# Two-layer hybrid decoder trunk on one core: the SBUF buffers get new start addresses

## The chip, the cores and the metric

The kernel runs on one core of a Trainium2 chip. The metric is the device time of one execution in microseconds (us). Two runs of the kernel before took 2884.22 and 2880.01 us, median 2882.11 us. A further, profiled execution took 2881.91 us, and its trace covers a span of 2880.1 us from the first to the last instruction.

## The reference

Two layers, sequence 256, model width 2048, everything in float32. Cut to what is computed:

```python
for l in range(2):
    u = rms_norm(x, g_mix[l])
    cq, ckv, xb, yb, gate_a, gate_r = split_columns(u @ w_in[l])   # 512, 576, 4 x 2048 columns
    attn = mla_branch(cq, ckv, ...)        # 16 heads, low-rank q and kv, rotary part, causal
    rec = rglru_branch(xb, yb, ...)        # conv4, 16 block-diagonal gates, linear scan, gelu
    x = x + (sigmoid(gate_a) * attn + sigmoid(gate_r) * rec) @ w_out[l]
    x = x + square(relu(rms_norm(x, g_mlp[l]) @ w_up[l])) @ w_down[l]      # 2048 -> 8192 -> 2048
    x = x + sigmoid(rms_norm(x, g_ple[l]) @ w_ple_gate[l]) * (p[l] @ w_ple_proj[l])
return rms_norm(x, g_final)
```

## The kernel before, in words

**Layout.** Activations stay in SBUF transposed: feature on the partition, the 256 positions along the free axis. `x` is `[128, 16, 256]` float32, 16 KiB a partition. `bufA` and `bufB` are `[128, 16, 2, 256]`, 32 KiB a partition each; index 2 chooses the high or the low part of an activation that was split in two (`hi` is the value rounded to the fp32r type, `lo` the remainder). They change roles from stage to stage: one holds the normalised input of a projection, the other the mixer's merged result or the MLP's hidden values.

**Weights.** The host lays all weights out as 1,004 "halves" of `[128, 1024]` float32. SyncE loads them in order into `raw` (6 buffers, lines 137 to 143). `split_half` (line 155) then makes two SBUF tiles of each: ScalarE copies `raw` into `hi` (line 160), VectorE computes `lo = raw - hi` (line 164). `hi` and `lo` have three buffers each, in the pool `wsp`. A half thus costs one ScalarE and one VectorE instruction, and feeds 24 matmuls.

**Products.** Each product of a weight block (the stationary operand, 128 columns, 512 bytes a partition) and an activation tile (the moving operand, 256 columns, 1,024 bytes a partition) is made as three fp32r matmuls: hi x hi, hi x lo, lo x hi. Two routines issue nearly all of them: `mm_both` (line 284 is its matmul; two output tiles at a time) and `mm3` (lines 259 to 261). Every matmul has a weight load of its own in front of it. Line 872 to 874 (the value projection `v`) is the one place where the roles are turned round: there the weights are the moving operand and the normalised latent `c1hi`/`c1lo` is the stationary one.

**Stages of a layer**, by the names that the trace shows as outputs: `c` and `kr` (the compressed q, kv and rope key), then eight head groups of `xb`, `yb`, `gr`, `k`, `v`, `q`, `qr`, `lru`, `ga` with the small attention matmuls `s` (scores), `pt` (transposes) and `o` (values) in between; `out`; four times `up` (16 tiles) and `down`; and `pg`/`pp`, the gated embedding. Between stages a norm issues a few matmuls of one column (`ms_...`, line 555) and one of 256 columns (`rb_...`, line 604).

**Order.** The program is emitted under a manual schedule: the order on each engine is fixed when the program is built, by a planner that carries costs of every step (`work`, `later`, `need`). Those costs do not depend on addresses.

**Where buffers lie.** Tile pools are placed one behind the other in the order in which they are opened, and the tiles of a pool in the order of their first allocation. Pool `const` comes first; its first tile starts at byte 16,512 of the partition, behind a reserved region and four small constants. So `x` starts at 16,512, and everything that follows takes its address from the sizes before it. All steps that the matmuls take from there (a tile of an activation 1,024 or 2,048 bytes, a block of a weight 512 bytes, a buffer 4,096 bytes) are multiples of 512 bytes, so an operand's address modulo 512 is that of its buffer.

Of the kernel before, what the change touches and what calls it, by code (L numbers as in the profile page):

```python
# [11 lines left out]
F32 = mybir.dt.float32  # L12
# [6 lines left out]
P = 128  # L19
S = 256  # L20
D = 2048
KT = D // P
DEPTH = 2
# [21 lines left out]
NPC = _c  # L45
# [8 lines left out]
def _parts(x, bits, n):  # L54

    out = []
    x = Fraction(x)
    for i in range(n):
        if x == 0:
            out.append(0.0)  # L60
            continue
        b = bits if i < n - 1 else 24
        m, e = math.frexp(float(x))
        q = Fraction(2) ** (e - b)
        v = Fraction(round(x / q)) * q
        out.append(float(v))
        x -= v
    return out


def _centered(x):
    x = x - math.floor(x)
    return x - 1 if x > Fraction(1, 2) else x
# [3 lines left out]
def trunk_kernel(ctx: ExitStack, tc: tile.TileContext, xT, pT, pos, par, gfin, invf, wu, out):  # L77
    nc = tc.nc

    const = ctx.enter_context(tc.tile_pool(name="const", bufs=1))  # L80
    wraw = ctx.enter_context(tc.tile_pool(name="wraw", bufs=6))
    wsp = ctx.enter_context(tc.tile_pool(name="wsp", bufs=3))
    tmp = ctx.enter_context(tc.tile_pool(name="tmp", bufs=6))
    att = ctx.enter_context(tc.tile_pool(name="att", bufs=1))
    tiny = ctx.enter_context(tc.tile_pool(name="tiny", bufs=4))
    banks = {
        t: (ctx.enter_context(tc.tile_pool(name=f"ps_{t}", bufs=n, space=PSUM)), n)
        for t, n in (("mm", 3), ("s", 2), ("t", 1), ("o", 1), ("r", 1))
# [120 lines left out]
    def later(key, *steps, deps=(), rank=1, also=()):  # L209

        job = Job((key, *also), rank, deps, steps)
        at = len(jobs)
        while at and jobs[at - 1].rank > rank:
            at -= 1
        jobs.insert(at, job)
# [126 lines left out]
        return tmp.tile([P, S], F32, tag="h", bufs=3, name=name)  # L342


    x = const.tile([P, KT, S], F32, name="x")

    bufA, bufB = (const.tile([P, KT, 2, S], F32R, name=n) for n in ("bufA", "bufB"))
    parT = const.tile([P, DEPTH * NPC], F32, name="parT")
    gf = const.tile([P, KT], F32, name="gf")
    nc.sync.dma_start(out=parT, in_=par)  # L350
    nc.sync.dma_start(out=x[:, 0:2, :], in_=xT[:, 0:2, :])
    load_to(0)
# [12 lines left out]
    make_identity(nc, ident)  # L365
    ones = const.tile([P, P], F32, name="ones")
    V.memset(ones, 1.0)
    power = const.tile([P, 4], F32, name="power")
    A.activation(power, ones[:, 0:4], AF.Copy, scale=-0.5)
    mask = const.tile([P, S], F32, name="mask")  # L370
    V.memset(mask[:, 0:P], 0.0)
# [2 lines left out]
    ropeS = const.tile([P, S], F32, name="ropeS")  # L374

    def rope_tables():
        fr = const.tile([P, 1], F32, name="invf")
        nc.sync.dma_start(out=fr, in_=invf)
        slots = []
        for n, tag in enumerate(("xch", "xcl", "vh", "vl")):  # L380
            w = att.tile([P, 512], F32, tag=tag, name=f"rope_w{n}")
            slots += [w[:, 0:S], w[:, S:512]]
        posi, ang, p2, p1, rem, turn, k, k2 = slots
        nc.sync.dma_start(out=posi.bitcast(I32), in_=pos.partition_broadcast(P))
        ops = []

        def ts(*a, **kw):
            ops.append(("V", 0.21, lambda: V.tensor_scalar(*a, **kw)))

        def tt(*a, **kw):  # L390
            ops.append(("V", 0.35, lambda: V.tensor_tensor(*a, **kw)))

        def rounded(o, src, by):
            ts(out=o, in0=src, scalar1=by, scalar2=ROUND, op0=ALU.mult, op1=ALU.add)
            ts(out=o, in0=o, scalar1=ROUND, scalar2=None, op0=ALU.subtract)

        def less(o, src, kk, c):
            ops.append(("V", 0.35, lambda: V.scalar_tensor_tensor(out=o, in0=kk, scalar=-c, in1=src, op0=ALU.mult, op1=ALU.add)))

        ops.append(("V", 0.21, lambda: V.tensor_copy(ang, posi.bitcast(I32))))  # L400
        ts(out=ang, in0=ang, scalar1=fr, scalar2=None, op0=ALU.mult)

        rounded(p2, ang, 2.0 ** -20)
        less(rem, ang, p2, 2.0 ** 20)
        rounded(p1, rem, 2.0 ** -10)
        less(rem, rem, p1, 2.0 ** 10)
        for n, (p, e) in enumerate(((p2, 20), (p1, 10))):
            c = _parts(_centered(Fraction(2) ** e / (2 * _PI)), 12, 3)
            if n == 0:
                ts(out=turn, in0=p, scalar1=c[0], scalar2=None, op0=ALU.mult)  # L410
            else:
                less(turn, turn, p, -c[0])
            rounded(k, turn, 1.0)
            less(turn, turn, k, 1.0)
            less(turn, turn, p, -c[1])
            less(turn, turn, p, -c[2])
        rounded(k, turn, 1.0)
        less(turn, turn, k, 1.0)
        c = _parts(2 * _PI, 12, 3)
        rounded(k2, rem, float(1 / (2 * _PI)))  # L420
        for v in c:
            less(rem, rem, k2, v)
        less(rem, rem, turn, -float(2 * _PI))
        rounded(k, rem, float(1 / (2 * _PI)))
        for v in c:
            less(rem, rem, k, v)
        ts(out=k, in0=rem, scalar1=3.1415925, scalar2=-3.1415925, op0=ALU.min, op1=ALU.max)

        ts(out=k2, in0=k, scalar1=-1.0, scalar2=None, op0=ALU.mult)
        tt(out=k2, in0=k, in1=k2, op=ALU.max)  # L430
        ts(out=k2, in0=k2, scalar1=-1.0, scalar2=math.pi / 2, op0=ALU.mult, op1=ALU.add)
        ops.append(("A", 1.0, lambda: A.activation(ropeS, k, AF.Sin)))
        ops.append(("A", 1.0, lambda: A.activation(ropeC, k2, AF.Sin)))

        for b in (0, 64):
            ts(out=ropeS[b:b + 32, :], in0=ropeS[b:b + 32, :], scalar1=-1.0, scalar2=None, op0=ALU.mult)
        later("rope", *ops, rank=1)


    cl = const.tile([P, DEPTH, 16], F32, name="cl")  # L440
    cl2 = const.tile([P, DEPTH, 16], F32, name="cl2")
    hba = const.tile([P, DEPTH, 16], F32, name="hba")
    hbx = const.tile([P, DEPTH, 16], F32, name="hbx")

    def lru_constants():
        work_ = t512("lru_c")
# [196 lines left out]

    PT = tuple(att.tile([P, 512], F32R, name=f"pt_{w}") for w in ("hi", "lo"))

    xbuf = att.tile([P, 2, 260], F32, name="xbuf")
    V.memset(xbuf[:, :, 0:4], 0.0)

    def split_steps(d, name, src, tag, cols=512):
# [35 lines left out]
    def mixer(l, u, mg, norm):  # L685
# [9 lines left out]
        for n in range(4):  # L695
            i, pr = divmod(n, 2)
            key = ("c", i, pr, l)
            ps = mm_pair(f"c{i}{pr}_{l}", key, u, hooks.get(n, ()))
            later(key, ("A", 0.6, lambda i=i, pr=pr, ps=ps: A.activation(dest(i, pr), ps, AF.Copy)), rank=-1)
            if l == n == 0:  # L700
                rope_tables()
                lru_constants()
            nl.squares((nl.name, "sq", n), lambda i=i, pr=pr: raw[i, pr], i, deps=(key,), last=pr == 1)
# [729 lines left out]
```

## Time and profile before

| | |
|---|---|
| median of 2 runs | 2882.11 us (2880.01 to 2884.22) |
| profiled execution | 2881.91 us, span 2880.1 us, mean granted TensorE clock 0.998 |
| TensorE matmul busy | 2853.1 us (99%), 24,800 matmuls |
| weight load busy | 2846.8 us (99%), 24,800 loads |
| VectorE busy | 1861.3 us (65%), 2,420 instructions |
| ScalarE busy | 1538.4 us (53%), 2,050 instructions |
| chain that ended last | 98% TensorE, 1% ScalarE |
| DMA | 535.43 MB, 186 GB/s, the weights' queue 55.6% of 16 engines' span |

How to read it: matmuls are pipelined and their ends are modelled, so that one is shown as 276 ns long while the next begins 113 ns after it. What a matmul costs the kernel is therefore the distance from its start to the next start, which this document calls the **step**. A window's count of matmuls gives it: a window of W us shows (W + 0.28) / step of them, since one that began up to 0.28 us before the window still reaches into it. The granted clock is a share of 2.4 GHz.

### The profile page before, as it was taken

Reading aid. Unit: us, or ns where it says so; the run is one execution under the profiler, and the core shown is the slowest. Engines: PE = TensorE matmul, PEld = TensorE weight load, DVE = VectorE, ACT = ScalarE, POOL = GpSimd, SP = SyncE. Lnnn points to the kernel's source line nnn. Section 1 sums busy time; section 2 is a strip of 40 time slices with the busy share of each in tenths; the row PEclk is TensorE's granted clock in tenths of the full one; section 3 lists DMA queues with packets and bytes.
Section 4 is the critical chain, followed back from the end, with each engine's and each line's share of the span. In section 5 each row is a group of like instructions: output and inputs, shape, how many; then the busy total and the mean of one; then the engine's idle time right before and its main releaser. Section 6 shows DMA issues by size and latency. Waiting matters only on the chain.

```text
span 2880.1 us, 60564 instructions
## 1 busy us (share of the span) xinstructions
PE 2853.1 (99%) x24800; PEld 2846.8 (99%) x24800; DVE 1861.3 (65%) x2420; ACT 1538.4 (53%) x2050; POOL 10.1 (0%) x17
## 2 busy tenths in 40 slices
PE   8999999999999999999999999999999999999998
PEld 8999999999999999999999999999999999999998
DVE  7877777765555555556758777777555555555665
ACT  5666666644444443444546666666453444434555
POOL 0000000000000000000000000000000000000000
PEclk9999999999999999999999999999999999999999
DMA  6555555555555555655555555555555555555553
GB/s 232 169 176 179 172 171 178 178 184 190 197 193 194 195 193 195 198 195 191 190 188 172 176 169 176 176 178 179 186 191 195 194 196 193 194 194 197 196 187 129
DMA packets 272583, 535.43 MB, mean 186 GB/s; under 512 B 30512, under 2 KB 30768, under 8 KB 272304
## 3 DMA queue, kind: packets, MB, share of 16 engines
q1 hardware_dynamic: 272304, 531.55, 55.6%
q8 instruction: 194, 3.18, 0.4%
q14 instruction: 85, 0.70, 0.1%
HBM read 529.33 MB, written 2.10 MB: 185 GB/s over the span
## 4 chain that ended last, share of the span: by engine, by line
PE 98%; ACT 1%; DVE 0%; DMA 0%; issue 0%; SPq 0%; ACTq 0%; POOLq 0%
PE up L284 24%; PE down L284 21%; PE yb L284 6%; PE gr L284 6%; PE xb L284 6%; PE out L284 5%; PE pg L284 5%; PE ga L284 5%; PE c L284 3%; PE down L259 1%; PE down L260 1%; PE down L261 1%; PE o L1040 1%; PE s L984 1%; PE v L872 1%; PE v L873 1%
## 5 line engine op out<-in xcount | busy, mean ns | idle before, releaser
L160 ACT ACTIVATE hi<-raw 128x1024 fp32r<-128x1024 f32 x1004 | 1065.7, 1061 | 1311.6 <-DMA raw<-wu 467.4
L164 DVE TENSOR_TENSOR lo<-raw,hi 128x1024 fp32r<-128x1024 f32 x1004 | 1229.5, 1225 | 808.1 <-ACT hi L160 786.0
L284 PE MATMUL up<-bufA,hi 128*128 128x256 f32 x2048 | 316.2, 276 | 0.0
L284 PE MATMUL up<-bufB,hi 128*128 128x256 f32 x2048 | 316.2, 276 | 0.0
L284 PE MATMUL down<-bufB,hi 128*128 128x256 f32 x1792 | 276.0, 276 | 0.0
L284 PE MATMUL down<-bufA,hi 128*128 128x256 f32 x1792 | 276.0, 276 | 0.0
L284 PEld LDWEIGHTS up<-bufA,hi 128*128 128x128 f32 x2048 | 270.6, 188 | 0.1
L284 PEld LDWEIGHTS up<-bufB,hi 128*128 128x128 f32 x2048 | 270.6, 188 | 0.1
L284 PEld LDWEIGHTS down<-bufB,hi 128*128 128x128 f32 x1792 | 236.4, 188 | 0.0
L284 PEld LDWEIGHTS down<-bufA,hi 128*128 128x128 f32 x1792 | 236.4, 188 | 0.0
L284 PE MATMUL up<-bufA,lo 128*128 128x256 f32 x1024 | 199.7, 276 | 0.0
L284 PE MATMUL up<-bufB,lo 128*128 128x256 f32 x1024 | 199.6, 276 | 0.0
L284 PE MATMUL down<-bufA,lo 128*128 128x256 f32 x896 | 174.5, 276 | 0.0
L284 PE MATMUL down<-bufB,lo 128*128 128x256 f32 x896 | 174.4, 276 | 0.0
L284 PEld LDWEIGHTS up<-bufA,lo 128*128 128x128 f32 x1024 | 154.4, 188 | 0.0
L284 PEld LDWEIGHTS up<-bufB,lo 128*128 128x128 f32 x1024 | 154.3, 188 | 0.0
L284 PEld LDWEIGHTS down<-bufA,lo 128*128 128x128 f32 x896 | 134.9, 188 | 0.0
L284 PEld LDWEIGHTS down<-bufB,lo 128*128 128x128 f32 x896 | 134.8, 188 | 0.0
L284 PE MATMUL xb<-bufB,hi 128*128 128x256 f32 x512 | 81.4, 281 | 0.0
L284 PE MATMUL yb<-bufB,hi 128*128 128x256 f32 x512 | 81.3, 281 | 0.0
L284 PE MATMUL yb<-bufA,hi 128*128 128x256 f32 x512 | 81.3, 281 | 0.0
L284 PE MATMUL xb<-bufA,hi 128*128 128x256 f32 x512 | 81.3, 281 | 0.0
(563 smaller groups left out, 5630.8 us busy)
## 6 DMA issues: line engine op xcount, KB each, us to landing
raw<-wu SPq DMA_DIRECT2D x1744, 256.0 KB, 3.0
raw<-wu SPq DMA_DIRECT2D x132, 512.0 KB, 3.3
y<-rows SPq DMA_DIRECT2D x4, 512.0 KB, 4.0
x<-xT SPq DMA_DIRECT2D x3, 512.0 KB, 7.5
x<-xT SPq DMA_DIRECT2D x2, 256.0 KB, 4.3
praw<-pT SPq DMA_DIRECT2D x2, 256.0 KB, 4.0
parT<-par SPq DMA_DIRECT2D x1, 184.0 KB, 2.5
rope_w<-pos SPq DMA_DIRECT2D x1, 128.0 KB, 4.4
```

The source lines that it names most:

```text
L160: A.activation(hi, src, AF.Copy)
L164: V.tensor_tensor(out=lo, in0=src, in1=f(hi), op=ALU.subtract)
L259: T.matmul(o, lhsT=wh, rhs=ah, start=start, stop=False, skip_group_check=shared)
L260: T.matmul(o, lhsT=wh, rhs=al, start=False, stop=False, skip_group_check=shared)
L261: T.matmul(o, lhsT=wl, rhs=ah, start=False, stop=stop, skip_group_check=shared)
L284: T.matmul(ps[:, t * S:(t + 1) * S], lhsT=w[:, (4 * t + kk) * P:(4 * t + kk + 1) * P], rhs=a, start=k == n == t == 0, stop=k == 15 and n = ...
L872: T.matmul(o, lhsT=ch, rhs=wh, start=k == 0, stop=False)
L873: T.matmul(o, lhsT=ch, rhs=wl, start=False, stop=False)
L984: T.matmul(o, lhsT=qr, rhs=kr["rot"][w][:, 0:n], start=False, stop=m == 1)
L1040: T.matmul(o[:, j * P:S], lhsT=v[:, j * S + t * P:j * S + (t + 1) * P], rhs=q[:, c], start=n == 0, stop=n == 5, skip_group_check=True,)
```

## The change

No instruction is added, removed or moved: with the buffers' numbers left out, the order of instructions and of waits is the same on every engine. Only start addresses differ. Two tiles without any instruction are added as spacers: `even` (32 bytes) and `pad` (256 bytes). The small tiles (parameters, constants of the recurrence, the convolution's buffer, the norms' and softmax's scratch) go to the front of SBUF.

```diff
+    small = ctx.enter_context(tc.tile_pool(name="small", bufs=1))
+    tiny = ctx.enter_context(tc.tile_pool(name="tiny", bufs=4))
+    even = ctx.enter_context(tc.tile_pool(name="even", bufs=1))
     const = ctx.enter_context(tc.tile_pool(name="const", bufs=1))
     wraw = ctx.enter_context(tc.tile_pool(name="wraw", bufs=6))
+
+    ctx.enter_context(tc.tile_pool(name="pad", bufs=1)).tile([P, 64], F32, name="pad")
     wsp = ctx.enter_context(tc.tile_pool(name="wsp", bufs=3))
     tmp = ctx.enter_context(tc.tile_pool(name="tmp", bufs=6))
     att = ctx.enter_context(tc.tile_pool(name="att", bufs=1))
-    tiny = ctx.enter_context(tc.tile_pool(name="tiny", bufs=4))
...
+    even.tile([P, 8], F32, name="even")
     x = const.tile([P, KT, S], F32, name="x")
     bufA, bufB = (const.tile([P, KT, 2, S], F32R, name=n) for n in ("bufA", "bufB"))
-    parT = const.tile([P, DEPTH * NPC], F32, name="parT")
-    gf = const.tile([P, KT], F32, name="gf")
+    parT = small.tile([P, DEPTH * NPC], F32, name="parT")
+    gf = small.tile([P, KT], F32, name="gf")
...
-    xbuf = att.tile([P, 2, 260], F32, name="xbuf")
+    xbuf = small.tile([P, 2, 260], F32, name="xbuf")
```

(`power`, `invf`, `cl`, `cl2`, `hba` and `hbx` move from `const` to `small` in the same way.)

What this does to the addresses, as the two built programs have them (bytes modulo 512):

| buffer | before | changed |
|---|---|---|
| `x`, `bufA`, `bufB` | 128 | 0 |
| `raw` (6 buffers, written by DMA) | 192 | 0 |
| `hi`, `lo` (3 buffers each) | 192 | 256 |
| `tmp` pool | 192 | 256 |
| `att` pool: `PT` | 192 | 256 |
| `att` pool: `c0`, `c1`, `k`, `q`, `v`, `xc`, ... | 224 | 256 |
| moving minus stationary operand, `mm_both` | -64 | 256 |
| the same for `k`, `q`, `qr`, `lru`, `pp` | +32 | 0 |
| the same for `v` | -32 | 0 |
| the same for the scores `s` | 0 | 0 |

## Rows read from the trace of the kernel before

**Rows 1.** The page: first lines, and the chain of waits.
```profile
span 2880.1 us, 60564 instructions
PE 2853.1 (99%) x24800; PEld 2846.8 (99%) x24800; DVE 1861.3 (65%) x2420; ACT 1538.4 (53%) x2050; POOL 10.1 (0%) x17
...
PE 98%; ACT 1%; DVE 0%; DMA 0%; issue 0%; SPq 0%; ACTq 0%; POOLq 0%
```

**Rows 2.** Waits of TensorE: us in total, times, longest.
```profile
PE c L284 <- ACT hi L160: 8.6, 1, 8.6
PE pt L1017 <- DVE p L1009: 2.6, 2, 1.3
```

**Rows 3.** Windows: us, then busy us and count per engine, clock, DMA share, GB/s.
```profile
553.00:640.00 87.00, 87.00 (x741) 87.00 (x741) 54.11 (x65) 42.75 (x54) 0.00 (x0) 1.00 0.56 187
654.00:662.00 8.00, 8.00 (x71) 8.00 (x70) 4.07 (x5) 2.25 (x4) 0.59 (x1) 1.00 0.51 184
664.00:720.00 56.00, 56.00 (x496) 56.00 (x495) 32.77 (x34) 27.86 (x33) 0.00 (x0) 1.00 0.58 189
720.00:1320.00 600.00, 600.00 (x5297) 600.00 (x5295) 332.10 (x321) 269.69 (x292) 0.00 (x0) 1.00 0.59 195
```

**Rows 4.** Groups by line, layer 0: count | busy us, mean ns | idle before.
```profile
L284 PE MATMUL yb<-bufA,hi 128*128 128x256 f32 x512 | 81.3, 281 | 0.0
L284 PE MATMUL xb<-bufA,hi 128*128 128x256 f32 x512 | 81.3, 281 | 0.0
L284 PE MATMUL gr<-bufA,hi 128*128 128x256 f32 x512 | 79.4, 277 | 0.0
L284 PE MATMUL ga<-bufA,hi 128*128 128x256 f32 x448 | 71.6, 282 | 0.0
L284 PE MATMUL out<-bufB,hi 128*128 128x256 f32 x448 | 71.0, 281 | 0.0
...
L874 PE MATMUL v<-hi,c1lo 128*128 128x256 f32 x64 | 18.0, 281 | 0.0
...
L259 PE MATMUL k<-c1hi,hi 128*128 128x256 f32 x64 | 17.9, 280 | 0.0
```

**Rows 5.** The page's groups of the MLP, and of the weight split.
```profile
L160 ACT ACTIVATE hi<-raw 128x1024 fp32r<-128x1024 f32 x1004 | 1065.7, 1061 | 1311.6 <-DMA raw<-wu 467.4
L164 DVE TENSOR_TENSOR lo<-raw,hi 128x1024 fp32r<-128x1024 f32 x1004 | 1229.5, 1225 | 808.1 <-ACT hi L160 786.0
L284 PE MATMUL up<-bufA,hi 128*128 128x256 f32 x2048 | 316.2, 276 | 0.0
...
L284 PE MATMUL down<-bufB,hi 128*128 128x256 f32 x1792 | 276.0, 276 | 0.0
```

**Rows 6.** Timeline of TensorE: first `v`, first `q` and first `gr` matmul of head group 4.
```profile
335.46 0.28 PE L872 MATMUL v<-hi,c1hi 128*128 128x256 f32 x1
...
338.30 0.28 PE L259 MATMUL q<-c0hi,hi 128*128 128x256 f32 x1
...
343.90 0.28 PE L284 MATMUL gr<-bufA,hi 128*128 128x256 f32 x1
```

**Rows 7.** Timeline of weight loads in front of matmuls of 128 columns: scores, transposes.
```profile
292.36 0.19 PEld L260 LDWEIGHTS s<-k_3l,q_3h 128*128 128x128 f32 x1
292.47 0.19 PEld L261 LDWEIGHTS s<-k_3h,q_3l 128*128 128x128 f32 x1
292.58 0.19 PEld L984 LDWEIGHTS s<-krk0h,qs 128*128 128x128 f32 x1
292.69 0.19 PEld L984 LDWEIGHTS s<-krk0l,qs 128*128 128x128 f32 x1
292.80 0.54 PEld L284 LDWEIGHTS gr<-bufA,hi 128*128 128x128 f32 x4
...
299.74 0.14 PEld L1018 LDWEIGHTS pt<-ident,p 128*128 128x128 f32 x1
299.85 0.14 PEld L1019 LDWEIGHTS pt<-ident,p 128*128 128x128 f32 x1
299.96 0.30 PEld L284 LDWEIGHTS ga<-bufA,hi 128*128 128x128 f32 x2
```

More of the change, by code (lines that the diff above doesn't have):

```diff
@@ L367, in trunk_kernel @@
     V.memset(ones, 1.0)
-    power = const.tile([P, 4], F32, name="power")
+    power = small.tile([P, 4], F32, name="power")
     A.activation(power, ones[:, 0:4], AF.Copy, scale=-0.5)
@@ L376, in rope_tables @@
     def rope_tables():
-        fr = const.tile([P, 1], F32, name="invf")
+        fr = small.tile([P, 1], F32, name="invf")
         nc.sync.dma_start(out=fr, in_=invf)
@@ L437, in rope_tables @@
         later("rope", *ops, rank=1)
[L440 to L443, printed above, removed]
+    cl = small.tile([P, DEPTH, 16], F32, name="cl")
+    cl2 = small.tile([P, DEPTH, 16], F32, name="cl2")
+    hba = small.tile([P, DEPTH, 16], F32, name="hba")
+    hbx = small.tile([P, DEPTH, 16], F32, name="hbx")
     def lru_constants():
```

## The prediction, made before the changed kernel was run

> **What bounds the kernel.** I read the page's first lines and its chain of waits first: TensorE is busy for 99% of the span and carries 98% of the chain [rows 1]. The waits of TensorE come next; the two longest sums are 8.6 and 2.6 us [rows 2], so data that come late cost next to nothing. The 24,800 matmuls are the time, and what one costs is its step, from start to start. So the third view is the windows, read for counts. In the steady MLP, 720 to 1320 us, 5,297 matmuls are shown in 600 us: (600 + 0.28) / 5297 = 113.3 ns. During `out`, 553 to 640 us, it is 87.28 / 741 = 117.8 ns [rows 3]. The granted clock is 1.00 in both, the 2.4 GHz level, and 256 columns at one a tick would be 106.7 ns. The question is what the 6.6 and 11.1 ns above that are, and whether addresses set them.
>
> Three things in the trace bear on it.
>
> *Two steps at one address.* `mm_both` reads with the same distance of moving and stationary operand (-64 modulo 512) in `out`, `xb`, `yb`, `gr`, `up` and `down`. Yet `out` steps at 117.8 and `down` at 113.3. The modelled length goes with it, 281 and 276 ns, which makes the groups readable: `xb`, `yb`, `out` are at 281, `up` and `down` at 276, `gr` at 277 [rows 4, 5]. The step is locked for hundreds of matmuls and changes only where another kind of matmul comes between: `up` still goes at 8.28 / 71 = about 117 ns before the norm's `rb` at 662 us, and 56.28 / 496 = 113.5 behind it [rows 3]. So there are two patterns in which loads and matmuls can settle, and the entry decides.
>
> *Other addresses, other steps.* From the first `v` at 335.46 to the first `q` at 338.30 there are 24 matmuls: 2.84 / 24 = 118.3 ns, with distance -32. From there to `gr` at 343.90 there are 48 (`q` 24, `qr` 12, `lru` 12): 5.60 / 48 = 116.7 ns, with distance +32 [rows 6]. Neither is 113.3 nor 117.8, with the same shapes and types.
>
> *The other engines do not matter.* Over those 600 us of MLP, VectorE is busy 332 and ScalarE 270 us, DMA moves 195 GB/s [rows 3], and every one of the 1,792 `down` matmuls in the group has the mean length of 276 ns [rows 5]. What disturbs a matmul's step is on TensorE itself: its two streams of reads, moving operand and next weights.
>
> **The change, part by part.** Spacers and moved small tiles issue nothing: 0 us. New addresses of `raw`, `x` and scratch touch DMA, ScalarE and VectorE. The two split instructions of a half take 1,061 and 1,225 ns [rows 5], against 24 x 113.3 = 2,720 ns of matmuls that the half feeds; in the MLP VectorE is busy 332 of 600 us [rows 3]. A change of some ten per cent in either is hidden there, and I cost it at 0. The mixer has less room; if that cover went, the bound would be the waits of TensorE, some us.
>
> What is left is the step. I take a ledger of what lies above 113.3 ns, the best step that any long stretch shows:
> - `out`: per layer 448 + 224 at line 284 and 96 at lines 259 to 261, so 1,536 in all, x 4.5 ns = 6.9 us.
> - `xb`, `yb`: 4 x 768 = 3,072 x up to 4.5 = 12 to 14 us (a few start at 113.3).
> - `k`, `q`, `qr`, `lru`: 1,152 x 3.4 = 3.9 us; `v`: 384 x 5.0 = 1.9 us.
> - `ga`, the first hundred `up` of each layer, `pp`, `pg`, `s` and bits of `c` and `gr`: about 6 us. The mean of 282 ns of `ga` against 276 [rows 4] contains waits that stay.
>
> Together about 32 us. What the new distance (256 for `mm_both`, 0 for `k`, `q`, `v`) does to the step, no row shows: it occurs nowhere but in the scores, five wide matmuls at a time. So I bound it.
>
> *Best end.* Weight loads in front of 128-column matmuls are not held up by a wide moving operand: they start 0.11 us apart, (292.80 - 292.36) / 4 and (299.96 - 299.74) / 2 = 110 ns, to within a few ns of rounding [rows 7]. A matmul of 256 columns needs one load, so 110 is the floor that rows give. Everything at 110 would be 32 us, plus some 24,000 wide matmuls x 3.3 = 79 us: 111 us off, 2771 us; with 109 and the row's rounding 2747 us.
>
> The Trainium skill ("TensorE: Matmul & The Clock Gate", section "Back-to-back issue gap") gives N / 2.4 + 2.5 ns for isolated warm matmuls, 109.2 ns at 256 columns, and says that in streams with loads both operations set the step. By its 109.2, all wide matmuls would sum to about 2750 us. No stretch of this trace reaches it.
>
> *Worst end.* The worst long step seen is 117.8 (118.3 in `v`). Of the 24,000 wide matmuls the ledger's items take some 7,000, so 17,000 now go at 113.3. If these went at 117.8: 17,000 x 4.5 = 76 us more, 2958 us. At 116.7 it would be 17,000 x 3.4 = 58, less 5 for `xb`, `yb`, `out`: 2935 us.
>
> *What I take.* The nearest row to the new main distance is the stretch that has both operands at multiples of 64 bytes, `mm_both` itself, and its commoner step is 113.3. The odd steps, 116.7 and 118.3, are those with an operand at 224, which is no multiple of 64; with the change none is left. I take 113.3 for all: 2881.9 - 32 = 2850 us. The profiled run is 0.2 us under the median of the runs, so nothing is added.
>
> **The rivals.**
> 1. *The step falls below 113.3.* The streams then no longer meet, and the loads' own rate is left. For: the step does depend on addresses [rows 6], and 3 ns a matmul lie between 113.3 and [rows 7]. Against: 113.3 does not vary over 600 us, as if it were the chain of one load behind one matmul's start, which no address shortens. Times: 2771 us at 110, 2810 us at 111.7.
> 2. *Slower: the MLP locks into the 117.8 pattern.* Now each MLP is set to 113.3 by one `rb` matmul at its start [rows 3]; nothing corrects it for some 680 us if the new distance settles otherwise there. For: both patterns exist at one address, and a distance of 256 puts the meeting of the two streams elsewhere in the matmul. Against: behind most short matmuls the kernel now settles at 113.3 (`gr` 277, `up`, `down` 276). It decides from a mean step of 117 ns on (57 us above now). If 12,000 MLP matmuls alone switch it is +54 us less what `xb`, `yb`, `out` gain; if all do, 2958 us, and if all go to 116.7, 2935 us.
> 3. *Nothing happens: 2882 us.* Then the step is a matter of phase alone, and the odd 116.7 of the alignment to 64 bytes, worth 6 us. The change does place `bufA` and the weights 256 apart, as the addresses show, but not the operands of `k`, `q` and `v`, which come to distance 0.
>
> The Trainium skill ("SBUF — State Buffer", section "Who interferes with whom") says that TensorE reads the moving operand and the weights through two independent ports and never waits for anyone; by that rule placement could not matter, which is rival 3, 2882 us. The trace disagrees in part, 116.7 and 118.3 against 113.3 at one shape, though two steps at one address fit no rule on addresses alone.
>
> **How the numbers follow.** Forecast, 113.3 nearly everywhere, 2835 to 2865 us: 0.29. Rival 1: 0.36 in its two prices (0.2 near 2771, 0.16 near 2810). Rival 2: 0.23, of which 0.18 near 2958 and beyond, and 0.05 near 2935. Rival 3, within 10 us of 2882: 0.12. A difference of 2% (58 us) is about what a measurement of this kernel can tell from no change: under 2824 us is faster, 0.36; over 2940 us slower, 0.18; between them 0.46. The likeliest single case gives 2850 us. The range goes from 2747, the floor of the loads, to 2958, the whole kernel at its worse step; what I leave out is a step above 117.8 and one below the loads' floor.
>
> **What would show it.** Counts in windows: the steady MLP at 5,297 per 600 us if its step stays, 5,460 at 110 ns, 5,097 at 117.8. The groups' mean length: `out`, `xb`, `yb` at 276 instead of 281 for the forecast, `up` and `down` at 281 for rival 2. `v` and `q` to `lru` should lose their 118.3 and 116.7. The counts of ScalarE and VectorE must stay, and TensorE's waits stay at some us. I am wrong if the MLP's step moves either way, for 12,000 of the wide matmuls are there.

## The result: 3007 us, slower by 4.3%

The changed kernel takes 3007.39 us (3006.45 and 3008.34) against 2882.11 us: a ratio of 1.0435, interval 1.039 to 1.048. That is slower, and beyond the upper end of the predicted range by 49 us. The profiled execution has a span of 3006.6 us against 2880.1, 126.5 us more, at the same granted clock of 0.998.

The page after, its first lines and the chain of waits, which answer to [rows 1]:

```profile
span 3006.6 us, 60564 instructions
...
PE 2980.5 (99%) x24800; PEld 2976.4 (99%) x24800; DVE 1863.5 (62%) x2420; ACT 1537.1 (51%) x2050; POOL 10.1 (0%) x17
...
PE 98%; ACT 1%; DMA 0%; DVE 0%; issue 0%; SPq 0%; ACTq 0%; POOLq 0%
```

Every count stands, VectorE and ScalarE are busy as long as before to within 2.2 us, and only TensorE's busy time (that of its matmuls, and with it that of its weight loads) grew, by 127 us. The waits of TensorE (us in total, times, longest) answer to [rows 2]:

```profile
PE c L289 <- ACT hi L165: 8.8, 1, 8.8
PE pt L1023 <- DVE p L1015: 2.4, 2, 1.2
```

They moved by 0.2 us each. So TensorE waits no longer for data; each matmul costs more. The windows of [rows 3] after the change (us, then busy us and count of TensorE, its loads, VectorE, ScalarE, GpSimd; clock, DMA share, GB/s):

```profile
553.00:640.00 87.00, 87.00 (x729) 86.97 (x728) 57.50 (x85) 46.86 (x67) 0.00 (x0) 1.00 0.54 176
654.00:662.00 8.00, 8.00 (x69) 8.00 (x68) 3.94 (x6) 3.41 (x4) 0.00 (x0) 1.00 0.48 156
664.00:720.00 56.00, 56.00 (x468) 55.95 (x467) 30.46 (x33) 24.97 (x29) 0.70 (x1) 1.00 0.54 181
720.00:1320.00 600.00, 600.00 (x5002) 600.00 (x5002) 309.65 (x293) 251.49 (x269) 0.00 (x0) 1.00 0.55 184
```

In the steady MLP the step is 600.28 / 5002 = 120.0 ns, 113.3 before. The window of 8 us shows 8.28 / 69 = 120.0 too, where it was 117. (The stages of this layer's end now lie 17 to 19 us later: the first window begins in the last `gr` and holds `ga`, the second holds the end of `out` and the first `up`, the third the norm's `rb`. The count in the third is therefore no step.) DMA moves 184 GB/s instead of 195: the same 535.43 MB are spread over a longer span.

The groups of layer 0 and of the split (count | busy us, mean ns of one | idle before), which answer to [rows 4, 5]:

```profile
L165 ACT ACTIVATE hi<-raw 128x1024 fp32r<-128x1024 f32 x1004 | 1063.1, 1059 | 1435.6 <-PE down L289 297.9
L169 DVE TENSOR_TENSOR lo<-raw,hi 128x1024 fp32r<-128x1024 f32 x1004 | 1229.9, 1225 | 889.8 <-ACT hi L165 878.7
L289 PE MATMUL up<-bufA,hi 128*128 128x256 f32 x2048 | 329.5, 283 | 0.0
...
L289 PE MATMUL down<-bufB,hi 128*128 128x256 f32 x1792 | 288.1, 283 | 0.0
...
L289 PE MATMUL yb<-bufA,hi 128*128 128x256 f32 x512 | 82.7, 284 | 0.0
...
L289 PE MATMUL out<-bufB,hi 128*128 128x256 f32 x448 | 72.0, 283 | 0.0
...
L878 PE MATMUL v<-hi,c1hi 128*128 128x256 f32 x64 | 18.1, 283 | 0.0
```

The split costs what it did. All kinds of matmul shown now have one length, 283 or 284 ns, where [rows 4, 5] had 276 to 282. And the first `v`, `q` and `gr` of head group 4 (start us, modelled us), as in [rows 6]:

```profile
346.57 0.28 PE L878 MATMUL v<-hi,c1hi 128*128 128x256 f32 x1
...
349.45 0.28 PE L264 MATMUL q<-c0hi,hi 128*128 128x256 f32 x1
...
355.21 0.64 PE L289 MATMUL gr<-bufA,hi 128*128 128x256 f32 x4
```

2.88 / 24 = 120.0 ns for `v`, 5.76 / 48 = 120.0 for `q` to `lru`: their 118.3 and 116.7 are gone, upwards.

**The sum.** Taken over the whole trace, from start to start, the matmuls of 256 columns that no wait follows (steps of 100 to 125 ns) are 24,173 before with a mean of 114.69 ns, 2772.3 us, and 24,154 after with 119.96 ns, 2897.5 us. That is 125.2 of the 126.5 us. After any disturbance the step is back at 120.0 within about eight matmuls; there is one pattern left, not two.

### The profile page after: what moved, and what is told of

Its sections match the earlier page's. It is cut to its first block, busy times and chain, and to the rows that moved or that the text cites. A ratio compares the mean times of both kernels' runs of the same rounds, so it can differ in the third digit from the quotient of the medians.

```text
span 3006.6 us, 60564 instructions
## 1 busy us (share of the span) xinstructions
PE 2980.5 (99%) x24800; PEld 2976.4 (99%) x24800; DVE 1863.5 (62%) x2420; ACT 1537.1 (51%) x2050; POOL 10.1 (0%) x17
## 2 busy tenths in 40 slices
DMA packets 272583, 535.43 MB, mean 178 GB/s; under 512 B 30512, under 2 KB 30768, under 8 KB 272304
## 4 chain that ended last, share of the span: by engine, by line
PE 98%; ACT 1%; DMA 0%; DVE 0%; issue 0%; SPq 0%; ACTq 0%; POOLq 0%
PE up L289 25%; PE down L289 21%; PE gr L289 6%; PE yb L289 6%; PE xb L289 6%; PE pg L289 5%; PE out L289 5%; PE ga L289 5%; PE c L289 3%; PE down L266 1%; PE down L265 1%; PE down L264 1%; PE o L1046 1%; PE q L266 1%; PE q L265 1%; PE q L264 1%
## 5 line engine op out<-in xcount | busy, mean ns | idle before, releaser
L289 PE MATMUL up<-bufA,hi 128*128 128x256 f32 x2048 | 329.5, 283 | 0.0
L289 PE MATMUL up<-bufB,hi 128*128 128x256 f32 x2048 | 329.5, 283 | 0.0
L289 PE MATMUL down<-bufB,hi 128*128 128x256 f32 x1792 | 288.1, 283 | 0.0
L289 PE MATMUL down<-bufA,hi 128*128 128x256 f32 x1792 | 288.1, 283 | 0.0
L289 PEld LDWEIGHTS up<-bufA,hi 128*128 128x128 f32 x2048 | 282.7, 192 | 0.1
L289 PEld LDWEIGHTS up<-bufB,hi 128*128 128x128 f32 x2048 | 282.7, 192 | 0.1
L289 PEld LDWEIGHTS down<-bufB,hi 128*128 128x128 f32 x1792 | 247.3, 192 | 0.0
L289 PEld LDWEIGHTS down<-bufA,hi 128*128 128x128 f32 x1792 | 247.3, 192 | 0.0
L289 PE MATMUL up<-bufA,lo 128*128 128x256 f32 x1024 | 206.3, 283 | 0.0
L289 PE MATMUL up<-bufB,lo 128*128 128x256 f32 x1024 | 206.3, 283 | 0.0
```

What stands on the lines that cost most here:

```text
L289: T.matmul(ps[:, t * S:(t + 1) * S], lhsT=w[:, (4 * t + kk) * P:(4 * t + kk + 1) * P], rhs=a, start=k == n == t == 0, stop=k == 15 and n = ...
```

## The experiments

The theory, called D: the step is set by the **distance** of moving and stationary operand, modulo 256 bytes rather than the 512 of the tables above, and distance 0 is the worst. Against it stood that the absolute places did it, that the moved small tiles did, or that the spacing repeats in 128 bytes. Each kernel is the changed one with spacers of other sizes, unless it says otherwise, and each time is that of a single execution, unless a number of runs is given; `pad2` is a spacer ahead of the `att` pool. A mean "of the whole trace" is taken as in the sum above.

**1. A distance of -64 everywhere for `mm_both`, as before, but with all other new places kept** (`k`, `q`, `lru` at +64, `v` at -64):

```diff
-    ctx.enter_context(tc.tile_pool(name="pad", bufs=1)).tile([P, 64], F32, name="pad")
+    ctx.enter_context(tc.tile_pool(name="pad", bufs=1)).tile([P, 16], F32, name="pad")
...
+    ctx.enter_context(tc.tile_pool(name="pad2", bufs=1)).tile([P, 16], F32, name="pad2")
```

> The changed kernel with the spacer before the weights cut from 256 to 64 bytes and a new one of 64 bytes ahead of scratch and attention buffers. Activations stay at multiples of 512; the distance moving minus stationary of mm_both is -64 again, as in the kernel before; k, q, lru get +64, v -64. Theory D (the distance of the two operands sets the step): mm_both back to the two steps of before, 113.3 or 117.8 ns, MLP at one of them; 2850 to 2960 us. Theory P (the place alone: activations at multiples of 512 bytes are slow): the step stays 120.0, 3007 us.

Measured: 2865.57 us, with the kernel before at 2884.07 beside it. Steady MLP (window, columns as above):

```profile
720.00:1320.00 600.00, 600.00 (x5297) 600.00 (x5296) 332.70 (x322) 269.20 (x290) 0.00 (x0) 1.00 0.59 195
```

The count of [rows 3] is back to the matmul, and TensorE's timeline at head group 4 reads:

```profile
333.09 0.29 PE L879 MATMUL v<-hi,c1hi 128*128 128x256 f32 x1
...
335.82 0.28 PE L265 MATMUL q<-c0hi,hi 128*128 128x256 f32 x1
...
341.26 0.64 PE L290 MATMUL gr<-bufA,hi 128*128 128x256 f32 x4
```

`v` 2.73 / 24 = 113.8 ns, `q` to `lru` 5.44 / 48 = 113.3. So 192 bytes less in one spacer, with 64 in `pad2`, are worth 142 us against the changed kernel; neither the small tiles at the front nor activations at multiples of 512 cost anything. It is not 113.3 everywhere: by the steps of the whole trace `k` locks at 117.8 and `gr` has a mean of 116.4 (113.7 before), while `out`, at 117.8 before, now has 113.3.

**2. Distance 128** (`pad` of `[P, 32]`, `pad2` of `[P, 32]`):

> Spacers of 128 and 128 bytes: mm_both at distance -128, k, q, lru at +128, v at -128. Theory D with a period of 256 bytes: 128 is not the bad distance, step between 113 and 118, 2850 to 2960 us. Theory D with a period of 128 bytes: 128 is the same as 0, 120.0 ns and 3007 us. Theory P: 120.0 ns, 3007 us.

Measured: 2977.62 us.

```profile
720.00:1320.00 600.00, 600.00 (x5059) 600.00 (x5058) 314.05 (x300) 255.34 (x272) 0.00 (x0) 1.00 0.57 186
```

600.28 / 5059 = 118.7 ns: neither 120.0 nor a return to 113.3. The pattern does not repeat in 128 bytes. The 118.7 is a mean: single steps go round a short sequence between 115 and 122 ns. The size can be worked out from the step alone: 2881.9 - 2772.3 = 109.6 us lie outside the wide steps, and 24,170 x 118.67 = 2868 us; the sum is 2978.

**3. Distance -192** (`pad` of `[P, 48]`, `pad2` of `[P, 8]`; `k`, `q`, `lru` at +32, `v` at -32):

> Spacers of 192 and 32 bytes: mm_both at distance -192 (64 if the period is 256), k, q, lru at +32 and v at -32 as in the kernel before. Theory D: k, q, lru at 116.7 and v at 118.3 again; mm_both somewhere between 113 and 118, 2850 to 2960 us; with a period of 128 the same steps as at -64, 113.3 and 117.8. Theory P: mm_both 120.0, 3007 us.

Measured: 2948.92 us.

```profile
720.00:1320.00 600.00, 600.00 (x5097) 600.00 (x5095) 317.65 (x304) 256.91 (x275) 0.00 (x0) 1.00 0.57 187
```

600.28 / 5097 = 117.8 ns, the second pattern of [rows 3], held through both MLPs. `gr` and `pg` go in part at 113.3 here (115.7 and 116.4 in the mean of the whole trace), so the distance of 64 allows both patterns with either sign. This is the mechanism of rival 2, at a distance other than the change's. In the mean of the whole trace `v` takes 118.4 and `q` to `lru` 116.7 ns, the odd steps of [rows 6] at the same +32 and -32. Their buffers lie at the same places modulo 512 as in the kernel before (192 and 224), so for these stages this run does not tell distance from place; experiment 5 does.

**4. Distance -32** (`pad` of `[P, 8]`, `pad2` of `[P, 40]`):

> Spacers of 32 and 160 bytes: mm_both at distance -32, k, q, lru at +160, v at -160. Theory D: mm_both at the 118.3 that v had at -32 in the kernel before, so some 2970 us; k, q, lru at 116.7 if the period is 128 (160 is then 32). Theory P: 120.0 ns, 3007 us.

Measured: 2970.79 us. The MLP's window, and the first `v` and `q` of head group 4:

```profile
720.00:1320.00 600.00, 600.00 (x5073) 600.00 (x5072) 314.76 (x300) 256.51 (x273) 0.00 (x0) 1.00 0.57 186
...
343.24 0.28 PE L879 MATMUL v<-hi,c1hi 128*128 128x256 f32 x1
...
346.12 0.28 PE L265 MATMUL q<-c0hi,hi 128*128 128x256 f32 x1
```

600.28 / 5073 = 118.3 ns, the mean step of `v` in [rows 6], found again in `mm_both`. The rest of the expectation did not come: `q`, `qr` and `lru`, at +160, do not take 116.7 but 118.7 ns in the mean of the whole trace, one more sign that 128 is no period, and `v`, at -160, takes 2.88 / 24 = 120.0, as slow as at distance 0.

**5. One spacer alone, put into the kernel before** (its small tiles and activations stay, activations at 128 modulo 512, weights now at 384, so the distance is -256):

```diff
     wraw = ctx.enter_context(tc.tile_pool(name="wraw", bufs=6))
+    ctx.enter_context(tc.tile_pool(name="pad", bufs=1)).tile([P, 48], F32, name="pad")
     wsp = ctx.enter_context(tc.tile_pool(name="wsp", bufs=3))
```

> The kernel before with nothing but a spacer of 192 bytes ahead of the split weights: activations stay at 128 modulo 512, hi and lo come to 384, so mm_both is at distance -256; k, q, lru stay at +32, v at -32. Theory D (distance modulo 256): mm_both at 120.0 ns, k, q, lru at 116.7, v at 118.3; about 3003 us. Theory P (multiples of 512, or the small tiles at the front, make it slow): 113.3 and 117.8 as before, 2882 us.

Measured: 3003.63 us, with the kernel before at 2878.82 (median of 7) beside it.

```profile
720.00:1320.00 600.00, 600.00 (x5002) 600.00 (x5001) 309.34 (x294) 251.24 (x267) 0.00 (x0) 1.00 0.56 184
```

The count of the changed kernel, 5,002, from a spacer of 192 bytes and nothing else. No address but those of the weights and what follows them was touched: the distance is the cause, not the multiple of 512. The weights' places alone are not it either: at 128 modulo 256 they gave 118.7 in experiment 2 and give 120.0 here. The first `k`, `v` and `q` of head group 4, at +32 and -32 as in the kernel before, with all their buffers 192 bytes further on:

```profile
342.44 0.28 PE L260 MATMUL k<-c1hi,hi 128*128 128x256 f32 x1
...
345.27 0.28 PE L873 MATMUL v<-hi,c1hi 128*128 128x256 f32 x1
...
348.11 0.28 PE L260 MATMUL q<-c0hi,hi 128*128 128x256 f32 x1
```

`v` keeps 2.84 / 24 = 118.3, and `q` to `lru` take 116.7 in the mean of the whole trace. `k`, for which 116.7 was expected as well, takes 2.83 / 24 = 117.9, here behind matmuls at 120.0. So at 32 bytes too what went before has a say.

**6. Distance -320** (`pad` of `[P, 80]`, `pad2` of `[P, 16]`), which is -64 less one more 256:

> The changed kernel with a spacer of 320 instead of 256 bytes before the weights and 64 before scratch: distance of mm_both -320, which is -64 if the period is 256. Theory D with a period of 256: the two steps 113.3 and 117.8, MLP at one of them, as at -64: 2866 us if the entry is as there. Period 512: another step, most likely 116 to 120, 2935 to 3007 us.

Measured: 2866.33 us, 0.8 us from the first experiment.

```profile
720.00:1320.00 600.00, 600.00 (x5297) 600.00 (x5296) 331.94 (x322) 269.90 (x290) 0.00 (x0) 1.00 0.59 194
```

Again 5,297 matmuls in the window. With 128 ruled out by experiment 2, the period is 256 bytes.

**7. Only the `lo` weights at distance 0** (`hi` stays at -64; `lo` gets a pool of its own):

```diff
+    ctx.enter_context(tc.tile_pool(name="pad", bufs=1)).tile([P, 16], F32, name="pad")
     wsp = ctx.enter_context(tc.tile_pool(name="wsp", bufs=3))
+    ctx.enter_context(tc.tile_pool(name="pad3", bufs=1)).tile([P, 48], F32, name="pad3")
+    wsl = ctx.enter_context(tc.tile_pool(name="wsl", bufs=3))
...
-        lo = wsp.tile([P, 1024], F32R, tag="lo", name=f"lo{h}")
+        lo = wsl.tile([P, 1024], F32R, tag="lo", name=f"lo{h}")
```

> hi at 64 and lo at 256 modulo 512, activations at 0: of six matmuls of mm_both four have their weights at distance -64 and two at -256. Theory D in the form that a matmul's moving reads meet the next matmul's load: the two steps beside a lo load near 120, four near 113.3 (or 117.8): mean 115.6 (118.5), so some 2900 us (2970). In the form that a matmul meets its own weights: the same mean, but the slow steps are those of the two lo matmuls themselves, one place later. If the pattern locks on the worst: all at 120, 3007 us.

Measured: 2956.56 us.

```profile
720.00:1320.00 600.00, 600.00 (x5097) 600.00 (x5096) 316.61 (x303) 257.30 (x276) 0.00 (x0) 1.00 0.57 187
```

Not what was expected. I had meant to see which matmuls of a product become slow, those with the bad load of their own or those that run while it is loaded for the next. Instead the long stretches of all stages go at 117.8 ns, and none at 113.3: a third of bad loads is enough to lock the whole sequence into the slower pattern. The steps do not add up matmul by matmul, and the question of own or next load stays open.

**8. The first experiment again, in four runs:**

> The kernel of run d64, timed against the kernel before: theory D and its single look say 2866 us, a ratio of 0.994; theory P is out already. If the state of the MLP were drawn anew in each execution, some runs would be 50 us longer.

Measured: 2865.87 us (2864.95 to 2866.71, 4 runs) against 2878.82 (2874.53 to 2883.91, 7 runs); ratio 0.9952, interval 0.9934 to 0.9969. With the distance at -64 instead of 256, the changed kernel is faster than the kernel before by half a per cent: little, but a ratio of 1 lies outside the interval. No run is 50 us longer, so the pattern that a stretch enters is not drawn anew in each execution.

**9. `k`, `q`, `lru` to +192, `v` to +64, `mm_both` at -64** (`pad2` of `[P, 48]`), to see whether another entry makes `gr` and `k` settle at 113.3:

> Activations at 0, weights at 64, scratch and attention buffers at 256 modulo 512: mm_both at -64 as in d64, k, q, qr, lru, pp at +192 (which is -64 modulo 256), v at -192 (+64). Theory D: only the two steps 113.3 and 117.8 anywhere except in the scores; since the distance no longer changes from yb to k, the pattern of 113.3 should go on through k (117.8 in d64): 2850 to 2866 us, ratio 0.990 to 0.995. If the entry into k switches to 117.8 all the same: 2866 us or a little more.

Measured: 2865.96 us (2864.92 to 2867.03, 4 runs) against 2881.99; ratio 0.9946, interval 0.993 to 0.9963: no gain over 8. `gr` kept its mixed mean, 116.5 ns over the whole trace. TensorE at head group 4:

```profile
334.25 0.28 PE L879 MATMUL v<-hi,c1hi 128*128 128x256 f32 x1
...
336.97 0.28 PE L265 MATMUL q<-c0hi,hi 128*128 128x256 f32 x1
...
342.62 0.63 PE L290 MATMUL gr<-bufA,hi 128*128 128x256 f32 x4
```

`v` 2.72 / 24 = 113.3 ns, `q` to `lru` 5.65 / 48 = 117.7 and `k` at 113.3, where experiment 1 had 113.3 for `q` to `lru` and 117.8 for `k`. At 64 bytes of distance both patterns exist, and a long stretch keeps the one that it entered: of the 58 unbroken stretches of at least 60 matmuls at one distance, in the kernel before and in each of experiments 1, 3, 6, 8 and 9, none holds both behind its first 27 matmuls.

**10 and 11. Fewer loads: hi x hi and hi x lo as one matmul of 512 columns**, at distance -64 and at 256. The matmul of 512 columns fills the whole PSUM bank that two output tiles share. These kernels leave out the separate sums of the two tiles, which run together in the bank; the columns that TensorE streams are as many as before:

```diff
-            for n, (w, a) in enumerate(((hi, ah), (hi, al), (lo, ah))):
-                for t in range(2):
-                    T.matmul(
...
+            aw = act[0][:, k, :, :].rearrange("p a s -> p (a s)")
+            for t in range(2):
+                c = slice((4 * t + kk) * P, (4 * t + kk + 1) * P)
+                T.matmul(ps, lhsT=hi[:, c], rhs=aw, start=k == t == 0, stop=False, skip_group_check=True)
+                T.matmul(ps[:, t * S:(t + 1) * S], lhsT=lo[:, c], rhs=ah, start=False, stop=k == 15 and t == 1, skip_group_check=True)
```

> Distance -64. In mm_both the products hi x hi and hi x lo are made as one matmul of 512 columns into the whole bank, lo x hi stays at 256 columns; the two output tiles are added into one bank, so the sums are not the reference's. 6,976 products go from three steps to one of 512 and one of 256 columns. Theory L (the distance slows the load that runs beside the moving reads; it costs time only where the moving operand is no longer than the load): 216 + 113, some 2789 us. Theory M (the distance slows the moving reads): the same here, 2789 us.

> The same edit at the changed kernel's distance of -256. Theory L: the step of 512 columns stays at 216 ns as at -64, since the load beside it has 100 ns to spare; the 256-column step is 120: 216 + 120, some 2840 us. Theory M: the 512-column step is longer than at -64 by twice what a 256-column step loses, 13 ns: 229 + 120, some 2930 us.

Measured: 2948.61 us at -64 and 2951.78 us at 256. The page at -64:

```profile
span 2946.8 us, 46614 instructions
## 1 busy us (share of the span) xinstructions
PE 2919.8 (99%) x17824; PEld 2590.9 (88%) x17824; DVE 1862.1 (63%) x2420; ACT 1536.3 (52%) x2050; POOL 10.1 (0%) x17
```

7,000 loads fewer, the load engine no longer full, and yet 83 us slower than with three short matmuls (experiment 1). Its timeline in `down`:

```profile
799.81 0.40 PE L291 MATMUL down<-bufB,hi 128*128 128x512 f32 x1
800.05 0.28 PE L292 MATMUL down<-bufB,lo 128*128 128x256 f32 x1
800.17 0.40 PE L291 MATMUL down<-bufB,hi 128*128 128x512 f32 x1
...
801.93 0.40 PE L291 MATMUL down<-bufB,hi 128*128 128x512 f32 x1
```

and that of the kernel at 256:

```profile
799.64 0.39 PE L290 MATMUL down<-bufB,hi 128*128 128x512 f32 x1
799.87 0.27 PE L291 MATMUL down<-bufB,lo 128*128 128x256 f32 x1
...
801.72 0.39 PE L290 MATMUL down<-bufB,hi 128*128 128x512 f32 x1
```

Six products take 2.12 us at -64, 353 ns each (235 for the wide matmul, 118 for the narrow), and 2.08 us at 256, 347 ns; other stretches at 256 have 353. Three steps of 113.3 would be 340, of 120.0 360. So both expectations missed, and neither theory, L or M, is borne out. Where one load in three is gone, the wide matmuls take 235 ns on average at either distance, and the 142 us between the distances shrink to 3. Only the last two of sixteen `down` and `out` tiles, which still go as three short matmuls, keep the old picture: at 256 they step at 120.0.

**What is settled, and what isn't.** The steps by distance modulo 256, from the windows and timelines above:

| distance | step, ns | x 2.4 GHz, ticks | where |
|---|---|---|---|
| 0 | 120.0 | 288 | the change, experiment 5 |
| 64, -64 | 113.3 or 117.8 | 272 or 282.7 | before, experiments 1, 3, 6, 8, 9 |
| 128 | 118.7 | 284.8 | experiment 2 |
| -32 | 118.3 | 284 | before, experiments 3 and 5 (`v`), 4 |
| +32 | 116.7, or 118.0 (`k` in 5) | 280 or 283 | before, experiments 3 and 5 (`k`, `q` to `lru`) |
| 96 | 120.0 | 288 | experiment 4 (`v`, at -160) |
| -96 | 118.7, or 118.0 (`k`) | 285 or 283 | experiment 4 (`k`, `q` to `lru`, at +160) |

The two rows of 96 rest on one run and on stretches of 24 and 48 matmuls at a time. Only 120.0 at distance 0 and 113.3 are one step repeated; the others are means over a sequence of unequal steps (at -32, from 115 to 123 ns).

Shown: the distance, with period 256, decides which steps are possible, at 64 and 32 bytes what went before decides among them, and the step sets the time. Argued only: that the moving reads and those of weight loads hold each other up inside TensorE. Not tried: distances in steps under 32 bytes, and an order of the program that enters every long run at 113.3.

## Why the prediction was wrong

**Right.** What bounds the kernel, and how to price it: the step times some 24,000 matmuls is 125.2 of the 126.5 us, the other engines and DMA cost nothing, and TensorE's waits stayed. Rival 3 fell. The Trainium skill ("SBUF — State Buffer", section "Who interferes with whom") says that TensorE reads through two independent ports and never waits for anyone. The measurement differs from what that would make of placement: one spacer of 192 bytes moved the kernel by 125 us (experiment 5). That one distance allows two locked patterns, 113.3 and 117.8, was read rightly from [rows 3] and showed again in experiments 1, 3 and 9.

**Wrong: "What I take".** I took 113.3 ns for the new distance, by way of the nearest row: both operands at multiples of 64 bytes. That alignment is not what counts. Distances of 0, 64 and 128 all keep it and give 120.0, 113.3 or 117.8, and 118.7. The term was 24,000 x 113.3; it measured 24,000 x 120.0, 160 us more, and 2850 + 160 = 3010 is the result within 3 us.

**Wrong: "Worst end".** I closed the range at 117.8 as the worst long step seen, and left out a step above it. But the new distance did occur in the trace of before: the scores have distance 0, as the table of the change says, and I set them aside as five matmuls at a time. These are the weight loads just ahead of the first row of [rows 7], each beside a score matmul of 256 columns:

```profile
292.00 0.19 PEld L984 LDWEIGHTS s<-krk0h,qs 128*128 128x128 f32 x1
292.12 0.19 PEld L984 LDWEIGHTS s<-krk0l,qs 128*128 128x128 f32 x1
292.24 0.19 PEld L259 LDWEIGHTS s<-k_3h,q_3h 128*128 128x128 f32 x1
```

With 292.36 from [rows 7] that is three intervals in 0.36 us: 120 ns each, the step of the whole changed kernel. I used the rows behind them, 110 ns apart, for the floor, and so read the good end from that place and not the bad one. That 256, the main distance, acts as 0 does no row of before showed, and the two score matmuls ahead of these went at 118 and 113 ns; but as a bound the row was there, and 24,000 matmuls at 120.0 instead of the forecast's 113.3 would have set the range's end near 2850 + 160 = 3010 us.

**Rival 2** had the right sign and its price went far enough only to 2958. It supposed a switch to the known slower pattern; what came is a third value with no second pattern beside it. The switch itself is real, in experiment 3, at 2949 us. **Rival 1** fell: no distance that was tried brought a long stretch of 256 columns under 113.3, so the 110 ns of loads before 128 columns is not a rate that these matmuls reach. The 109.2 ns of the Trainium skill ("TensorE: Matmul & The Clock Gate", section "Back-to-back issue gap"), given there for isolated matmuls, stayed out of reach of every long stretch in every run.

## What to carry to other kernels

Where matmuls with loads run back to back, read the step from counts, and look at the distance of moving and stationary operand modulo 256 bytes: here -64 gave 2866 us and 0 gave 3007, with the same instructions, and one spacer tile decides it. A distance of 64 is no guarantee: the kernel before had it with 2882 us, and experiment 3, which entered the slower pattern, took 2949. Aligning all buffers to one round number is what puts the distance at 0. And when a change makes a rare condition the common one, price it from the rare condition's own rows, however few, before a commoner row that only looks alike.

## What the runs showed of the hardware

- The step of a 256-column fp32r matmul with a load of its own is not one number: 113.3, 116.7, 117.8, 118.3, 118.7 and 120.0 ns at a granted clock of 1.00, by start addresses alone, and at 64 and 32 bytes by what went before too.
- A pattern, once entered, holds for thousands of matmuls: 5,097 in 600 us without a change in experiment 3, at a distance where 113.3 is also possible.
- A 512-column matmul took 235 ns, 564 ticks at 2.4 GHz for 512 columns, with the loads busy 88% of the span; taking loads away made the kernel slower by 83 us (experiment 10 against 1).
- With a third of the weights at distance 0 and the rest at 64, all long stretches went at 117.8 ns (experiment 7).
